# Layer 1's adaLN vectors contracted lane by lane on VectorE during the first MLP

## The chip, the cores and the metric

One NeuronCore of a Trainium2 chip runs the whole kernel. The metric is the device time of one execution in microseconds (us).

## What is computed

A two-layer diffusion block works on 512 latent tokens and 256 context tokens of 1024 features. Layer 0 mixes tokens with gated linear attention (4 heads, two directions), layer 1 with neighbourhood attention (16 heads), and each layer ends with a gated MLP (2816 hidden features, a width-3 convolution on one branch). Every sub-layer is modulated by adaLN vectors. Cut to what matters here:

```python
sc_lat, sc_ctx = silu(c), silu(c_ctx)                # two conditions of 1024 features
for i in range(2):
    mod_l = sc_lat @ ada_w[i] + ada_b[i]             # ada_w[i]: 1024 x 6144, six vectors of 1024
    mod_c = sc_ctx @ ada_w[i] + ada_b[i]
    sh1, s1, g1, sh2, s2, g2 = split(mod, 6)         # for the latents and for the context
    h = rms_norm(x) * norm1_g * (1 + s1) + sh1;  x = x + g1 * mixer(h)
    h = rms_norm(x) * norm2_g * (1 + s2) + sh2;  x = x + g2 * conv_ffn(h)
```

In layer 1 the context only feeds keys and values: of its six vectors it needs the first two. Everything is float32 in and out. Large products are made exact enough from pairs of float32r tiles (a high and a low part of each operand, three matmuls for one).

## The kernel before

The work goes through five stages on one core: the first norms and adaLN vectors (0 to about 60 us), gated linear attention with its output projection (to about 490), the MLP of layer 0 (to about 1035), neighbourhood attention (to about 1410), the MLP of layer 1. The code is a list of steps; each instruction goes to the engine that the code names, and a list scheduler orders every engine's queue by the order of the code, letting a later instruction go ahead where by its own model of the times the earlier one is not ready. Tiles come from pools with a fixed number of buffers by tag; a load is issued when a buffer of its tag comes free, all loads from SyncE's one queue (SP).

**adaLN vectors.** `ada_first` makes layer 0's first two. The other ten come from `ada_step(l, m, i)` (L152): a quarter of the contraction of vector m of layer l, which is two K-tiles of 128 input features. For each K-tile a tile `sa` of 128x1024 weights (512 KB) is loaded (L159; two buffers, shared by all of them), and four float32 matmuls (L161), each over 256 columns with the 32 columns of `cs` as weights, go to four groups of 32 columns of the array and so to four groups of 32 rows of one PSUM bank `aux`. Only two of the 32 columns of `cs` carry anything (the two conditions). The profile has each of these float32 matmuls as two records, so a K-tile is 8 records of L161. After the fourth quarter ScalarE copies 256 columns out (`rows`, L166), two transposes (L171) turn them feature major, and VectorE adds the bias (`ada_use`, L114).

**Where the steps stand.** `part_a(h)` (L603) is the first part of an attention head, called the level part here: seven levels of decay products (VectorE L491 to L498, matmuls L469), after each of the first five a group of 24 value and gate matmuls (`vr_group`), and after each level one `ada_step`. The list `blocks` (L670) has 28 of them: layer 0's vectors 2 to 5, then layer 1's vectors 0 to 2. `part_b(h)` (L618), the state part, makes the key decay (L519, L521), the key transposes (L531), the states (L542) and the outputs (L578), and between them the next head's query and key projections (`qk_group`, 24 matmuls each); at its end stands one more `ada_step` in heads 0 to 2 (L654). Head 3 has four in its level part. In the neighbourhood attention (L999 to L1065) another twelve `ada_step` calls make layer 1's vectors 3 to 5, two in each of five pairs of heads and two among the last output products.

**Weights.** `wunit` (L189) loads 128x1024 weights into `st` (L193; three buffers), ScalarE rounds them into `wh` (L200) and VectorE subtracts for `wl` (L201); five pairs of buffers.

**The MLP of layer 0** (`ffn`, L723): 22 tiles of 128 hidden features, in six groups of three and one of four. `in_tile(j)` (L763) runs the two input products over all 768 tokens (96 matmuls), and `finish` (L782) makes the convolution on VectorE (L788 to L790), the gate's SiLU on ScalarE, the gated product (L796) and the split into `uh`, `ul` (L217, L218). After a group the output products of its tiles are summed for each token tile in PSUM (`mm`, three buffers), and VectorE multiplies by the gate and adds to the residual (L293, L294). The first two tiles of the MLP are run together by `in_first` (L770).

Of the kernel before, what the change touches and what calls it, by code (L numbers as in the profile page):

```python
# [16 lines left out]
KD = 8  # L17
# [15 lines left out]
# row ranges of the packed small vectors  # L33
# [5 lines left out]
def body(ctx, tc, x, ctx_x, small, ada0, ada, w_gla, a_w1, a_w2, gn, w_go, w_fi, w_fo,  # L39
# [19 lines left out]
    # ---------------------------------------------------------------- constants  # L59
# [30 lines left out]

    sT = cst.tile([128, 384], F32, name="sT")
# [5 lines left out]
    # ---------------------------------------------------------------- adaLN vectors  # L97
# [11 lines left out]
    def ada_use(l, o, n, src):  # L109
        """Feature tiles o..o + n of layer l's adaLN vectors, from their products with the conditions."""  # L110
# [14 lines left out]
    def ada_first(q, pool):  # L125
        """256 columns (two feature tiles) of the first two adaLN vectors of layer 0; returns what is left to do."""
# [25 lines left out]
    def ada_step(l, m, i):  # L152
        """Quarter i of the contraction of adaLN vector m of layer l; returns what is left to do with it."""
# [21 lines left out]

    def gate_rows(pool, l, n, j):
# [11 lines left out]
    # ---------------------------------------------------------------- helpers  # L188
    def wunit(src, gate=None, eng=None):  # L189
        """1024 columns of weights (times a gate for each) as an exact pair of float32r tiles."""  # L190
# [29 lines left out]
    # the features that the projections read, as pairs of float32r: one place for all sub-layers  # L220
# [4 lines left out]
    def affine(i, dst, src, l, n, k, j):  # L225
        """dst = src * A + B of feature tile k, on the engine that i picks."""
# [6 lines left out]
    def normed(pool, xt, g=None, cut=(0, 512, 1024), **at):  # L233
        """xt / rms(xt) (times g), as two halves of the features."""
# [22 lines left out]
    def norm_pair(pool, l, n, t, c0, blocks=False, **at):  # L257
        """Modulated norm of token tiles t and t + 1, feature major, into columns c0.. of H; returns
        the part that TensorE begins."""
# [36 lines left out]
    # ================================================================ layer 0, GLA  # L296
# [44 lines left out]
    with tc.tile_pool(name="gla", bufs=6) as pool:  # L341
# [22 lines left out]
        # w2 as rows of (high, high, low) parts against the rows (high, low, high) of the low-rank features  # L364
# [98 lines left out]
        def blocks_of(kk, qq, w, flip):  # L463
            """Products of w keys by w queries, of the same block or (flip) of its neighbour; keys on partitions."""
# [92 lines left out]
        def silu_r(h, c):  # L557
            """norm_g * silu(r) of one chunk, with the exponential's table."""
# [44 lines left out]
        def part_a(h, extra=None):  # L603
            vr_group(h, 0)
            diag(h)
            for i in range(7):
# [8 lines left out]
                if extra and i >= 5:  # L615
                    extra(i - 5)

        def part_b(h, fill):  # L618
            """fill: up to eight callables of other work, one after each step."""
            fill = list(fill) + [None] * 8  # L620

            def other(i):
# [545 lines left out]
```

## Time and profile before

| | us |
|---|---|
| median of 3 runs | 1770.52 |
| lowest and highest run | 1769.62, 1773.61 |
| profiled execution: its span, the only time given for it | 1771.4 |
| TensorE busy | 1719.7 (97%) |
| VectorE busy | 1037.1 (59%) |
| ScalarE busy | 663.7 (37%) |
| GpSimd busy | 319.7 (18%) |

The page shows the slowest core, here the only one. PE is TensorE, PEld its weight loads, DVE VectorE, ACT ScalarE, POOL GpSimd, SP the queue of loads. Matmuls are pipelined, so the records of two neighbours overlap: what one costs is read from start to start. PEclk is the clock granted to TensorE as a share of full speed.

### The profile page before, as it was taken

What the parts mean: (1) busy time and instruction counts of PE and PEld (TensorE: products, weight loads), DVE (VectorE), ACT (ScalarE), POOL (GpSimd) and SP (SyncE); (2) the same over time, 40 slices, a digit from 0 to 9 for tenths busy, and PEclk for the clock granted to TensorE, in tenths of its full rate; (3) what the DMA queues carried; (4) which work ended last, traced back from release to release, by engine and by line L of the source; (5) the groups of instructions that cost most, each with busy time, mean ns of one, the idle gap of its engine ahead of it and who ended that gap; (6) DMA issues with size and microseconds to landing.
All of it is one profiled execution on the core that took longest, in us unless ns stands there. A gap on an engine that the chain in (4) does not pass through costs nothing.

```text
span 1771.4 us, 27345 instructions
## 1 busy us (share of the span) xinstructions
PE 1719.7 (97%) x11099; PEld 1451.4 (82%) x11099; DVE 1037.1 (59%) x1599; ACT 663.7 (37%) x1225; POOL 319.7 (18%) x474
## 2 busy tenths in 40 slices
PE   6999999999999999999999999999999999999998
PEld 4767676777798999989899978888888788888887
DVE  4697767774646455564655484445445565556555
ACT  4575646552441211212122254443434432233222
POOL 2042323221100000000000023433443202222221
PEclk9999999999999999999999999999999999999999
DMA  8553525331121211212212122133232232333331
GB/s 288 154 192 120 191 84 191 93 111 72 49 95 60 72 60 48 79 59 66 63 57 72 60 66 70 50 100 103 98 107 73 84 106 80 101 107 106 92 100 48
DMA packets 50446, 169.36 MB, mean 96 GB/s; under 512 B 6608, under 2 KB 8528, under 8 KB 50320
## 3 DMA queue, kind: packets, MB, share of 16 engines
q1 hardware_dynamic: 50320, 167.62, 29.3%
q8 instruction: 87, 1.43, 0.3%
q14 instruction: 39, 0.32, 0.1%
HBM read 163.40 MB, written 2.10 MB: 93 GB/s over the span
## 4 chain that ended last, share of the span: by engine, by line
PE 80%; DVE 9%; ACT 3%; issue 2%; DMA 2%; POOL 2%; SPq 0%; DVEq 0%; POOLq 0%; ACTq 0%
PE mm L205 18%; PE mm L206 17%; PE mm L207 17%; PE aux L205 6%; PE aux L207 6%; PE aux L206 6%; PE mm L962 2%; PE aux L945 2%; PE aux L920 2%; DVE t L498 1%; PE aux L161 1%; DVE t L497 1%; PE aux L578 1%; DVE t L492 1%; PE aux L542 1%
## 5 line engine op out<-in xcount | busy, mean ns | idle before, releaser
L205 PE MATMUL mm<-hh,wl 128*128 128x384 f32 (+3 forms) x976 | 344.0, 353 | 3.8 <-ACT hh L217 2.8
L206 PE MATMUL mm<-hl,wh 128*128 128x384 f32 (+3 forms) x976 | 340.6, 349 | 0.4 <-DVE hl L218 0.4
L207 PE MATMUL mm<-hh,wh 128*128 128x384 f32 (+3 forms) x976 | 340.6, 349 | 0.0
L200 ACT ACTIVATE wh<-st 128x1024 fp32r<-128x1024 f32 (+1 forms) x197 | 204.0, 1052 | 317.7 <-issue 179.5
L201 DVE TENSOR_TENSOR wl<-st,wh 128x1024 fp32r<-128x1024 f32 (+1 forms) x196 | 242.7, 1244 | 65.0 <-ACT wh L200 43.0
L205 PEld LDWEIGHTS mm<-hh,wl 128*128 128x128 f32 (+1 forms) x976 | 183.5, 188 | 23.6 <-ACT hh L217 3.5
L206 PEld LDWEIGHTS mm<-hl,wh 128*128 128x128 f32 (+1 forms) x976 | 183.9, 188 | 20.5 <-issue 4.2
L205 PE MATMUL aux<-hh,wl 128*128 128x384 f32 (+2 forms) x576 | 200.5, 348 | 0.0
L207 PE MATMUL aux<-hh,wh 128*128 128x384 f32 (+2 forms) x576 | 200.2, 348 | 0.0
L206 PE MATMUL aux<-hl,wh 128*128 128x384 f32 (+2 forms) x576 | 200.2, 348 | 0.0
L207 PEld LDWEIGHTS mm<-hh,wh 128*128 128x128 f32 (+1 forms) x976 | 184.0, 189 | 15.0
L205 PE MATMUL mm<-wh,ul 128*128 128x512 f32 (+1 forms) x444 | 175.1, 395 | 0.0
L206 PE MATMUL mm<-wl,uh 128*128 128x512 f32 (+1 forms) x444 | 173.7, 391 | 0.0
L207 PE MATMUL mm<-wh,uh 128*128 128x512 f32 (+1 forms) x444 | 172.8, 391 | 0.0
L197 POOL TENSOR_TENSOR st<-st,gB 128x512 f32<-128x512 f32 x60 | 92.6, 1572 | 269.2 <-DMA st<-in 177.5
L788 DVE TENSOR_SCALAR tt<-apad,sT 128x769 f32<-128x769 f32 (+1 forms) x44 | 32.3, 734 | 166.7 <-ACT apad L759 166.7
L245 POOL TENSOR_SCALAR ms<-ss 128x1 f32<-128x1 f32 x26 | 8.8, 340 | 621.0 <-ACT xn L243 620.3
L205 PE MATMUL mm<-wh,hl 128*128 128x512 f32 x288 | 117.7, 409 | 2.3 <-ACT wh L200 1.7
L206 PE MATMUL mm<-wl,hh 128*128 128x512 f32 x288 | 116.0, 403 | 0.0
L205 PEld LDWEIGHTS aux<-hh,wl 128*128 128x128 f32 x576 | 108.3, 188 | 8.9 <-issue 1.8
L207 PE MATMUL mm<-wh,hh 128*128 128x512 f32 x288 | 115.7, 402 | 0.0
L206 PEld LDWEIGHTS aux<-hl,wh 128*128 128x128 f32 x576 | 108.5, 188 | 7.5 <-issue 0.4
(200 smaller groups left out, 2779.4 us busy)
## 6 DMA issues: line engine op xcount, KB each, us to landing
st<-in SPq DMA_DIRECT2D x196, 512.0 KB, 3.6
sa<-in SPq DMA_DIRECT2D x82, 512.0 KB, 4.2
sx<-in SPq DMA_DIRECT2D x14, 512.0 KB, 5.7
xl<-in SPq DMA_DIRECT2D x8, 512.0 KB, 7.7
xc<-in SPq DMA_DIRECT2D x4, 512.0 KB, 4.7
out<-xn SPq DMA_DIRECT2D x8, 256.0 KB, 2.0
raw<-in SPq DMA_DIRECT2D x16, 96.0 KB, 2.4
t<-q SPq DMA_DIRECT2D x16, 64.0 KB, 3.6
```

The source lines that it names most:

```text
L161: mm(ps[32 * j:32 * j + 32, 0:256], cs[:, k, :], st[:, 256 * j:256 * j + 256], start=k == 0, stop=k == KD - 1, skip_group_check=True)
L197: nc.gpsimd.tensor_mul(st[:, s_], st[:, s_], gate[half])
L200: nc.scalar.activation(hi, st, AF.Copy)
L201: (eng or nc.vector).tensor_sub(lo, st, hi.bitcast(F32))
L205: mm(out, a[1], b[0], start=first, stop=False)
L206: mm(out, a[0], b[1], start=False, stop=False)
L207: mm(out, a[0], b[0], start=False, stop=last)
L492: nc.vector.tensor_sub(v(eq)[:, :, 0, :], v(bB)[:, :, 0, :], cB)
L788: nc.vector.tensor_scalar(tt, ap_[:, 1:1 + m], cw[1], cb, OP.mult, OP.add)
L920: mm(pss[hh][:, off:off + 256], qe[a_][p_, 128 * t:128 * t + 128], ke[b_][p_, ks], start=i == 0, stop=i == 2)
L945: nc.tensor.transpose(pT[:, i * 128:(i + 1) * 128], S2[:, o:o + 128], ident)
L962: mm(po[64 * hh:64 * hh + 64, 128 * t:128 * t + 128], V[:, vs[i], 64 * hh:64 * hh + 64], PTs[hh][:, i * 128:(i + 1) * 128], start=i == 0, ...
```

## The change

- Layer 1's twelve steps in the linear attention and twelve in the neighbourhood attention are removed. Layer 0's sixteen stay; a level part now has a step after its first six levels while there are any left (6, 6, 4), and the state part has none.
- New `ada_lanes(pool, l, m, c)`: eight steps, one for each K-tile. A step loads one `sa` tile and lets VectorE multiply it by the condition's value of the lane (the partition) and add it to an accumulator `acc` of 128x1024 (one buffer). The eighth step adds up the 128 lanes with one group of four float32 matmuls against `one0` (a column of ones and 31 of zeros), and goes on as `ada_step` did: copy, two transposes, bias.
- The MLP of layer 0 has a list of eight such jobs: vectors 0 and 1 for the latents and for the context, vectors 2 to 5 for the latents, 64 steps in all. Each `in_tile` runs four of them at its end, so that they fill tiles 2 to 17.
- The MLPs' pool has four instead of five buffers for tags without a number of their own.

```diff
+    one0 = cst.tile([128, 32], F32, name="one0")
+    nc.gpsimd.memset(one0, 0.0)
+    nc.gpsimd.memset(one0[:, 0:1], 1.0)
...
+    def ada_lanes(pool, l, m, c):
+        acc = [None]
+
+        def step(k):
+            if k == 0:
+                acc[0] = pool.tile([128, 1024], F32, name="acc", tag="acc", bufs=1)
+            st = ast.tile([128, 1024], F32, name="sa", tag="sa")
+            nc.sync.dma_start(st, ada[6 * l + m - 2, k])
+            if k == 0:
+                nc.vector.tensor_scalar(acc[0], st, cs[:, k, c:c + 1], None, OP.mult)
+            else:
+                nc.vector.scalar_tensor_tensor(acc[0], st, cs[:, k, c:c + 1], acc[0], OP.mult, OP.add)
+            if k < KD - 1:
+                return
+            ps = ps_aux()
+            for j in range(4):
+                mm(ps[32 * j:32 * j + 32, 0:256], one0, acc[0][:, 256 * j:256 * j + 256], start=True, stop=True,
+                   skip_group_check=True)
+            rows = sml.tile([128, 256], F32, name="rows", tag="rows", bufs=1)
+            nc.scalar.activation(rows, ps[:, 0:256], AF.Copy)
+            pm = ps_aux()
+            for f in range(2):
+                nc.tensor.transpose(pm[:, f * 128:(f + 1) * 128], rows[:, f * 128:(f + 1) * 128], ident)
...
+        return [lambda k=k: step(k) for k in range(KD)]
...
-                todo = ada_step(*blocks.pop(0)) if h < HEADS - 1 or i < 4 else None
+                todo = ada_step(*blocks.pop(0)) if blocks and i < 6 else None
...
-            if h < HEADS - 1:
-                ada_step(*blocks.pop(0))()
...
-        blocks = [(0, m, i) for m in range(2, 6) for i in range(4)] + [(1, m, i) for m in range(3) for i in range(4)]
+        blocks = [(0, m, i) for m in range(2, 6) for i in range(4)]
...
-        with tc.tile_pool(name=f"ffn{l}", bufs=5) as pool:
+        with tc.tile_pool(name=f"ffn{l}", bufs=4) as pool:
...
-                return finish(j, [in_group(j, 1, w1, rng) for rng in rngs])
+                u = finish(j, [in_group(j, 1, w1, rng) for rng in rngs])
+                for job in jobs[:4]:
+                    job()
+                del jobs[:4]
+                return u
...
+            jobs = []
+            if l == 0:
+                for m, c in ((0, 0), (0, 1), (1, 0), (1, 1), (2, 0), (3, 0), (4, 0), (5, 0)):
+                    jobs += ada_lanes(pool, 1, m, c)
...
-        later = [(1, m, i) for m in range(3, 6) for i in range(4)]
...
-            if 1 < pr < 7:
-                ada_step(*later.pop(0))()
...
-                if t in (1, 2):
-                    ada_step(*later.pop(0))()
```

## Rows read from the trace of the kernel before

**Rows 1.** The page: the span, and the busy time of each engine with its share of the span and its instructions.
```profile
span 1771.4 us, 27345 instructions
PE 1719.7 (97%) x11099; PEld 1451.4 (82%) x11099; DVE 1037.1 (59%) x1599; ACT 663.7 (37%) x1225; POOL 319.7 (18%) x474
```

**Rows 2.** Busy time by stretch: from:to and length, then busy us (instructions) of PE, PEld, DVE, ACT and POOL, the granted clock, the DMA engines' busy share and GB/s. State part of head 0, level and state part of head 1, of head 2, level part of head 3.
```profile
124.60:160.60 36.00, 35.62 (x202) 30.16 (x201) 24.77 (x35) 17.86 (x34) 9.50 (x14) 1.00 0.52 174
160.60:200.30 39.70, 37.56 (x466) 26.80 (x465) 38.95 (x64) 25.62 (x57) 12.07 (x12) 1.00 0.39 122
200.30:249.10 48.80, 45.08 (x337) 37.68 (x337) 25.81 (x38) 22.76 (x44) 10.75 (x16) 0.93 0.45 150
249.10:288.20 39.10, 37.05 (x464) 26.38 (x463) 38.33 (x63) 25.58 (x57) 13.79 (x12) 1.00 0.38 118
288.20:335.70 47.50, 44.32 (x340) 37.16 (x339) 25.96 (x39) 22.73 (x44) 10.74 (x16) 0.96 0.47 159
335.70:375.10 39.40, 37.57 (x455) 27.22 (x454) 38.72 (x64) 25.60 (x57) 12.04 (x12) 1.00 0.34 108
```

**Rows 3.** The chain that ended last, in order of time (start, us, what): where head 1's state part and head 2's level part begin.
```profile
200.26 0.87 DVE t L519
...
249.12 1.73 DVE b L415 x2
```

**Rows 4.** TensorE's instructions in order of time around the start of head 1's state part: start, us, engine, line, operation, out<-in, shape, count, and in brackets the idle time before it and what ended it.
```profile
205.03 0.44 PE L205 MATMUL mm<-hh,wl 128*128 128x384 f32 x1
...
207.73 0.34 PE L205 MATMUL mm<-hh,wl 128*128 128x384 f32 x1
211.79 1.08 PE L161 MATMUL aux<-sa,cs 128*32 128x256 f32 x8 [3.72 <-DMA sa<-in]
...
213.29 0.52 PE L207 MATMUL mm<-hh,wh 128*128 128x384 f32 x1
213.61 0.52 PE L205 MATMUL mm<-hh,wl 128*128 128x384 f32 x1
...
216.84 0.42 PE L531 MATMUL aux<-ident,t 128*128 128x128 f32 x1
```

**Rows 5.** The same for head 2, from the fifth step of its level part to its key transposes.
```profile
284.88 1.07 PE L161 MATMUL aux<-sa,cs 128*32 128x256 f32 x16
285.89 0.50 PE L205 MATMUL mm<-wh,hl 128*128 128x512 f32 x1
...
291.99 0.39 PE L161 MATMUL aux<-sa,cs 128*32 128x256 f32 x1
...
292.86 0.64 PE L469 MATMUL aux<-t,t 128*32 128x32 f32 x48
293.43 0.44 PE L205 MATMUL mm<-hh,wl 128*128 128x384 f32 x1
...
299.61 0.77 PE L161 MATMUL aux<-sa,cs 128*32 128x256 f32 x8 [3.13 <-DMA sa<-in]
...
303.96 0.71 PE L531 MATMUL aux<-ident,t 128*128 128x128 f32 x5
```

**Rows 6.** The queue of loads (SP) at the same place of head 1: start, us from the first issue to the end of the last, line, what is loaded, count.
```profile
204.26 2.33 SPq L193 DMA_DIRECT2D st<-in  x2
206.69 1.31 SPq L159 DMA_DIRECT2D sa<-in  x2
```

**Rows 7.** Busy time by stretch, columns as in rows 2: the 7 us after the wait, and the 30 after them.
```profile
211.80:218.80 7.00, 7.00 (x37) 4.85 (x38) 0.00 (x0) 1.36 (x4) 1.65 (x3) 0.55 0.74 248
218.80:248.80 30.00, 30.00 (x161) 26.13 (x160) 14.40 (x25) 12.36 (x27) 3.54 (x8) 1.00 0.33 109
```

**Rows 8.** TensorE's instructions in order of time, columns as in rows 4: a K-tile between projection matmuls, and a pair of adaLN transposes.
```profile
352.27 0.40 PE L207 MATMUL mm<-wh,hh 128*128 128x512 f32 x1
352.50 0.40 PE L205 MATMUL mm<-wh,hl 128*128 128x512 f32 x1
352.83 0.64 PE L161 MATMUL aux<-sa,cs 128*32 128x256 f32 x8
353.40 0.50 PE L206 MATMUL mm<-wl,hh 128*128 128x512 f32 x1
353.74 0.40 PE L207 MATMUL mm<-wh,hh 128*128 128x512 f32 x1
...
1392.53 0.38 PE L171 MATMUL aux<-ident,rows 128*128 128x128 f32 x2
...
1392.98 0.40 PE L207 MATMUL mm<-wh,oh 128*128 128x512 f32 x1
```

**Rows 9.** Busy time by stretch, columns as in rows 2: one pair of heads of the neighbourhood attention, and its end with the last norms.
```profile
1260.00:1304.00 44.00, 44.00 (x333) 35.32 (x335) 19.42 (x44) 15.01 (x33) 16.59 (x28) 1.00 0.27 88
...
1380.00:1410.00 30.00, 27.15 (x175) 21.24 (x174) 19.60 (x35) 14.45 (x32) 5.31 (x12) 1.00 0.33 106
```

**Rows 10.** The same for a group of three tiles of the first MLP: its input products, and its output products.
```profile
563.00:616.00 53.00, 53.00 (x303) 52.43 (x302) 24.97 (x33) 16.58 (x24) 0.00 (x0) 1.00 0.25 80
616.00:638.00 22.00, 22.00 (x96) 17.75 (x95) 15.68 (x23) 0.30 (x1) 0.00 (x0) 1.00 0.07 24
```

**Rows 11.** The instructions of L789 and of L788: engine, operation, out<-in, count, ns least/median/most, first and last start, shapes. The shorter durations belong to the 512 columns of the second MLP, the medians to 769.
```profile
L789 DVE SCALAR_TENSOR_TENSOR tt<-apad,sT,tt x44: 740/1021/1804, 515.2 to 1738.5; 128x769 f32<-128x769 f32 x22, 128x512 f32<-128x512 f32 x22
...
L788 DVE TENSOR_SCALAR tt<-apad,sT x44: 540/682/1537, 514.5 to 1737.9; 128x769 f32<-128x769 f32 x22, 128x512 f32<-128x512 f32 x22
```

**Rows 12.** VectorE's instructions in order of time at the end of the first group's input products, columns as in rows 4.
```profile
541.63 0.95 DVE L218 TENSOR_TENSOR ul<-u,uh 128x768 fp32r<-128x768 f32 x1
543.63 1.39 DVE L293 TENSOR_TENSOR tmp<-mm,gB 128x512 f32<-128x512 f32 x2 [1.06 <-PE mm L207]
```

**Rows 13.** The transfers of tile `sa`, all 82, from issue to landing.
```profile
DMA to landing us min/median/max: 3.3/4.2/6.3
```

More of the change, by code (lines that the diff above doesn't have):

```diff
@@ L174, in ada_step @@
         return turn
+    ada_jobs = []
+    def ada_lanes(pool, l, m, c):
[20 more added lines that the diff above has]
+                nc.tensor.transpose(pm[:, f * 128:(f + 1) * 128], rows[:, f * 128:(f + 1) * 128], ident)
+            o = 8 * m
+            mod = modT[l][:, o:o + 8, c]
+            bias = sT[:, R_AB + 48 * l + o:R_AB + 48 * l + o + 8]
+            nc.vector.tensor_add(mod.rearrange("p (j i) -> p j i", i=2),
+                                 pm[:, 0:256].rearrange("p (i j s) -> p j i s", i=2, j=4)[:, :, :, 0],
+                                 bias.rearrange("p (j i) -> p j i", i=2))
+            if m in (1, 4):
+                i = 0 if m == 1 else 1
+                r = (R_N1, R_N2)[i] + 8 * l
+                nc.vector.scalar_tensor_tensor(modA[l][:, 8 * i:8 * i + 8, c], mod, 1.0, sT[:, r:r + 8], OP.add,
+                                               OP.mult)
+        return [lambda k=k: step(k) for k in range(KD)]
     def gate_rows(pool, l, n, j):
@@ L1046, in body @@
             values(pr, 2)
-            if 1 < pr < 7:
-                ada_step(*later.pop(0))()
             turn(pr, 3)
@@ L1063, in body @@
                     rest()
-                if t in (1, 2):
-                    ada_step(*later.pop(0))()
     fgB = []
```

## The prediction

> **What bounds the kernel now.** I read the page's busy line first: TensorE is busy for 97% of the span, VectorE for 59% [rows 1]. So a matmul that goes away should be worth its own time, unless the stage it leaves is one of the few that another engine paces. The next view, the busy time stretch by stretch, finds that exception. Each linear-attention head has two parts. In its level part (heads 1 to 3: 39.7, 39.1 and 39.4 us) VectorE is busy for 38.95, 38.33 and 38.72 us, and the length is the same whether seven contraction steps run in it (heads 1 and 2) or four (head 3): VectorE paces it. In the state part TensorE paces, and the lengths differ: 36.0 us in head 0, 48.8 in head 1, 47.5 in head 2 [rows 2]. The boundaries are the start of the gate scan (L415) and of the key decay (L519) [rows 3].
>
> The instructions of TensorE in order of time say why heads 1 and 2 are longer. At 205.03 head 1 begins the first 24 projection matmuls of the next head; the seventh contraction step of part_a stands in the middle of them, its weights are not there, and TensorE waits 3.72 us. Then matmuls start 0.32 us apart (213.29 to 213.61) until, at 216.84, the first key transpose can go [rows 4]. The same happens in head 2: 3.13 us, and the transposes begin at 303.96 [rows 5]. The DMA queue shows the cause: the two transfers of that step were issued at 206.69, behind two weight loads (`st`) of which the second was held [rows 6]. And the granted clock was 0.55 in the 7 us after the wait, 1.00 afterwards [rows 7]: 1.2 instead of 2.4 GHz for most of them. In the neighbourhood attention and in the MLP TensorE is busy without a gap at a clock of 1.00 [rows 9, 10].
>
> **The change, part by part.** Time is counted against the profiled span, 1771.4 us; the page gives no other time of that execution, and the median of the runs, 1770.52, lies 0.9 lower.
>
> *What a contraction step costs on TensorE.* A K-tile of a step is 8 records of L161. Alone between projection matmuls it stretches two starts from 352.50 to 353.74, 1.24 us, where two pitches of 0.23 would be 0.46: 0.78 us. Without the changeovers it is 0.57 us (352.83 to 353.40) [rows 8]; two in a row take 1.01 us (284.88 to 285.89) [rows 5]. A step is two K-tiles: 1.0 to 1.6 us, and I take 1.2.
>
> *Linear attention.* Twelve of 28 steps go (layer 1's first three vectors), and the 16 left run in the first six levels of heads 0 to 2: 6, 6 and 4 instead of 8, 8, 8 and 4.
> - Head 0 loses its seventh step and the one at the end of the state part, both where TensorE paces: 2 x 1.2 = 2.4 us.
> - Head 1 loses the same two. Without the first the 24 matmuls (the first 16 go out from 205.03 to 207.73, 0.18 apart) end at 205.03 + 24 x 0.18 = 209.3, so the transposes start 7.5 us earlier than 216.84: 3.7 us of wait, the rest contraction and slow clock. With the last step, 1.2: 8.7 us.
> - Head 2 keeps four. Two of the three removed from its level part lie ahead of the transposes' matmuls (those from 284.88 and 291.99); without them the seventh level's products, now at 292.86, are over at 291.4 instead of 293.43, and 24 matmuls end at 295.7: 8.3 us before 303.96. With the last step: 9.5 us.
> - Head 3 loses four steps in a part that VectorE paces: 0.
>
> Sum 20.6 us. The bounds: 8 us if a wait like the two comes back elsewhere, 22 if head 3 gives a little. VectorE also loses three bias additions there, too short to count.
>
> What the slow clock does is in the term as rows show it. The Trainium skill, "TensorE: Matmul & The Clock Gate", section "HAM oscillation — how this bites in real kernels", tells the same story of a wait for a transfer that drops the clock, and its rule would also turn against the change: contraction work that filled gaps in the level parts is gone. By the rows those gaps do not matter: with 2.1 of 39.1 us idle in head 2 and 1.8 of 39.4 in head 3 the clock stayed at 1.00 [rows 2]. By the rule it could fall in head 3, which would idle 1.8 + 4 x 1.2 = 6.6 us; the sum of 20.6 would then shrink by what the rival of the clock, below, is priced at.
>
> *Neighbourhood attention.* Twelve steps go where TensorE is busy 44.00 of 44.00 us [rows 9]. Eleven x 1.2 = 13.2; the twelfth stands among the last norms, where TensorE has 2.85 us idle of 30 [rows 9], and counts 0. Six transposes: a pair takes 1392.98 - 1392.53 - 0.23 = 0.22 us [rows 8], 0.7 for three vectors. Sum 13.9 us, bounds 11 and 17.
>
> *First MLP, on TensorE.* Eight jobs (six vectors for the latents, two for the context), each with one group of four matmuls of the form of a K-tile, 0.78, and two transposes, 0.22: 8 x 1.0 = 8.0 us added; nothing hides them, as TensorE has no gap there [rows 10].
>
> *First MLP, on VectorE.* 64 steps over 128x1024 values. L789 is the same operation: 1.02 us for 769 columns and 0.74 for 512, so 1.09 ns a column, and 1024 take 1.30 us; the first of each job, by L788 (0.68 and 0.54), 0.82 [rows 11]. A group of three tiles lasts 75 us and has VectorE busy 40.7 [rows 10]; twelve steps add 15 us: 56 of 75. On the average it fits. GpSimd is idle there [rows 10], so nothing of its work is in the way.
>
> *The transfers.* 64 loads of 512 KB replace 48, through the same two buffers and the same queue, where a transfer takes 4.2 us (3.3 to 6.3) from issue to landing [rows 13]. Two at a time give a step every 2.7 us or so; eight need about 25 us, and a job has two tiles, 33 us, without the output products. What stands behind a waiting step on VectorE are the gated products and splits of the tile (L796, L218), the weight splits (L201) and the additions to the residual (L293, L294); behind a waiting load on the queue, the next `st`. The weights are converted well ahead of use, and the additions have three PSUM buffers, so the tender place is the end of a group: the last split ends at 541.63 + 0.95 = 542.6, and the first output sum is done at 543.6 [rows 12], a margin of 1 us. A step of 1.3 us that has just started there costs up to 0.3 us, with a wait for its transfer 2 to 3. Seven such places, and the two norms beside them: bounds 0 and 15 us, none below, since nothing in that stage is removed. I take 3, as VectorE is free a good third of the time and most steps will be over by then.
>
> *The pool of the MLP, four buffers instead of five,* and the new tiles: nothing, covered by the same gaps; if that cover failed, it would show as waits of the norms, within the bounds just given.
>
> The sum: 20.6 + 13.9 - 8.0 - 3 = 23.5 us. 1771.4 - 23.5 = 1747.9, and 0.9 less for the median: 1747 us, 1.3% faster.
>
> **The rivals.**
> - *The wait comes back.* Layer 0's remaining steps still queue their transfers behind `st` loads, and the sixth step of head 1 or one of head 2 could be the late one; or the weights of the next head become late once the transposes come earlier. For it: the cause sits in the queue, and the queue stays. Against it: the sixth step of head 2, at 291.99, had its data in time [rows 5]. The linear attention then gives 8 us or so, the rest as above: 1760.
> - *The clock falls in the level parts.* Less filler in heads 2 and 3, TensorE idles, and 144 value and gate matmuls of a head at 0.23 become 0.46 for part of the time. If a quarter of them in each of two heads runs at half speed, 2 x 36 x 0.23 = 17 us come back: 1764. Against it: the 1.00 of those parts now.
> - *VectorE becomes the bound of the MLP: slower.* A VectorE that waits inside its queue for a transfer is lost to the tile. With y us for a step and its wait, a group needs 40.7 + 12 y. Beyond y = 2.9 that exceeds 75 us, and the groups are paced by it; the time is longer than before once each of 5.3 groups loses over 5 us, from y = 3.3 on. With 1.3 of work and 2.1 of wait (half of a transfer's 4.2, as two run at a time) y is 3.4, a group loses 6.5 and all 35; the gain of 34.5 less 8.0 is 26.5. That gives 1771.4 + 35 - 26.5 - 0.9 = 1779. For it: the steps are issued just behind one another in every tile, and only two buffers feed them. Against it: it needs every step to wait in full, though the loads depend on nothing but a free buffer and can run ahead of the tile.
>
> **How the numbers follow.** The forecast has 0.62, the returning wait 0.16, the clock 0.09, VectorE as the bound 0.13. Likeliest 1747. The forecast alone ranges from 1738 (no stall, upper bounds of both attention terms) to 1755 (stalls of 10). To leave out only the slower case and some of the clock's, the range is 1738 to 1764. A measurement of this kernel can tell 0.2%, 3.5 us, from no change. Faster by more than that: the first three cases, nearly whole, 0.86; slower: 0.11; within: 0.03.
>
> **What would show it.** Right: no wait of TensorE for `sa` at the start of the state parts of heads 1 and 2, a clock of 1.00 there, state parts of some 38 to 40 us; level parts still 39 us; neighbourhood attention shorter by 14 us; no L161 after head 2; the MLP longer by 8 to 12 us with VectorE busy some 56 of 75. Wrong: waits of TensorE on L218, L796 or L293 at every group's end, idle time of VectorE ahead of the lane steps that `sa` ended, level parts at a lower clock, or a wait for `sa` or `st` as long as the two removed.

## The result and the profile after

The changed kernel takes 1756.19 us (median of 4 runs, 1750.43 to 1757.60) against 1770.07 beside it: a ratio of 0.9909, with a 95% interval of 0.9893 to 0.9925. The ratio stands for 16 us less, 0.9%, where 1747 and 1.3% were forecast; the two medians lie 13.9 us apart, and the same kernel measured once more (the last experiment) has 0.9902, 17 us. The profiled execution took 1755.54 us. Its span stands against [rows 1] as follows: TensorE lost 316 matmul records, VectorE gained 67 instructions.

```profile
span 1753.8 us, 26851 instructions
PE 1695.0 (97%) x10783; PEld 1442.9 (82%) x10783; DVE 1107.6 (63%) x1666; ACT 663.1 (38%) x1227; POOL 331.8 (19%) x476
```

**Where the time went, stage by stage.** I measured each stage from one fixed instruction to another, in both traces: the first gate scan of a head, the first key transpose, the first matmul of the gate rows behind head 3 (L182, now L227), and the first convolution step (L788, now L835) of the first and the last MLP tile.

| stretch | before, us | after, us | change | forecast |
|---|---|---|---|---|
| head 0's scan to gate rows (linear attention) | 339.4 | 322.1 | -17.3 | -20.6 |
| of it, head 0's scan to its key transposes | 48.8 | 48.8 | 0.0 | -1.2 |
| key transposes of head 0 to head 1 | 87.5 | 81.9 | -5.6 | -8.7 |
| head 1 to head 2 | 87.1 | 77.4 | -9.7 | -9.5 |
| head 2 to head 3 | 90.7 | 88.8 | -1.9 | -1.2 |
| first MLP, first to last tile | 484.4 | 500.6 | +16.2 | +11.0 |
| from there to the same place of the second MLP's start | 419.1 | 405.7 | -13.4 | -13.9 |

The forecast column of the second to fifth lines divides the terms by the instant at which each removed step stood: the last step of a head's state part stands behind its own key transposes. The first line and the last two sum to -14.5; the rest of the 17.6 us between the spans is 1.7 us ahead of the first scan and 1.4 us between gate rows and MLP. Those are differences between executions: kernels below that leave these parts as they were (e1, e2) have the second as well, and over all runs the first scan starts anywhere from 78.4 to 82.6 us.

**The linear attention.** Busy time by stretch (columns as in rows 2), to be laid beside [rows 2]; the boundaries are again scans and key decays, but the list scheduler orders them a little differently, so lengths can't be compared to the microsecond.

```profile
160.70:197.00 36.30, 34.19 (x440) 25.34 (x439) 35.45 (x58) 24.43 (x52) 16.19 (x12) 1.00 0.35 113
197.00:243.90 46.90, 43.80 (x362) 37.81 (x362) 29.20 (x44) 23.94 (x50) 13.09 (x20) 0.96 0.33 105
243.90:279.70 35.80, 34.21 (x394) 24.59 (x393) 35.51 (x58) 24.05 (x51) 12.99 (x9) 1.00 0.36 119
279.70:325.90 46.20, 42.33 (x344) 37.42 (x343) 28.64 (x42) 23.56 (x49) 13.86 (x20) 0.96 0.26 81
```

The level parts of heads 1 and 2 keep VectorE busy throughout (35.45 of 36.30, 35.51 of 35.80), and their clock is 1.00 with six and four contraction steps in them. The state parts have not become 38 to 40 us, and their clock is 0.96. TensorE's instructions at the place of [rows 4] show why:

```profile
201.43 0.34 PE L251 MATMUL mm<-hl,wh 128*128 128x384 f32 x1
203.93 0.69 PE L175 MATMUL aux<-ident,rows 128*128 128x128 f32 x2 [2.15 <-ACT rows L170]
...
205.35 0.69 PE L252 MATMUL mm<-hh,wh 128*128 128x384 f32 x1
205.83 0.52 PE L250 MATMUL mm<-hh,wl 128*128 128x384 f32 x1
...
209.53 1.47 PE L576 MATMUL aux<-ident,t 128*128 128x128 f32 x12
```

The wait of 3.72 us for `sa` is gone; the key transposes start at 209.53 instead of 216.84. But another wait stands a few microseconds earlier: 2.15 us for `rows`, which ScalarE copies out of PSUM (L170) before the adaLN transposes. Two projection matmuls behind it start 0.48 us apart (205.35 to 205.83), where 0.17 is usual here. The copy itself starts at 203.51; ScalarE has no wait of its own in the 6 us ahead of it, only other work, weight copies (L245) among it. At the place of [rows 5], head 2:

```profile
286.93 1.47 PE L576 MATMUL aux<-ident,t 128*128 128x128 f32 x12
...
288.59 0.34 PE L252 MATMUL mm<-hh,wh 128*128 128x384 f32 x1
291.92 1.63 PE L587 MATMUL aux<-V,t 128*128 128x256 f32 x4 [2.99 <-ACT t L577]
```

Here the transposes start 17 us earlier than at 303.96, and the next thing is late: the state matmuls (L587) wait 2.99 us for the copies of the transposed keys (L577), again on ScalarE. Its own instructions there:

```profile
288.25 0.40 ACT L608 ACTIVATE er<-er 128x256 f32<-128x256 f32 x1
289.82 0.42 ACT L610 ACTIVATE er<-er 128x256 f32<-128x256 f32 x1 [1.17 <-DVE er L609]
290.15 0.47 ACT L479 ACTIVATE q<-mm 128x384 f32<-128x384 f32 x1
290.52 1.62 ACT L577 ACTIVATE t<-aux 128x512 f32<-128x512 f32 x4
```

The copies start at 290.52, 3.6 us after the transposes began. Ahead of them in ScalarE's queue stood a gate operation (L610) that itself waited 1.17 us for VectorE (L609).

**The first MLP.** At the end of a group of tiles, VectorE's instructions in order of time, the place that [rows 12] showed:

```profile
671.44 1.28 DVE L195 SCALAR_TENSOR_TENSOR acc<-sa,cs,acc 128x1024 f32<-128x1024 f32 x1
672.63 1.08 DVE L843 TENSOR_TENSOR u<-tt,aux 128x256 f32<-128x256 f32 x3
675.01 1.28 DVE L195 SCALAR_TENSOR_TENSOR acc<-sa,cs,acc 128x1024 f32<-128x1024 f32 x1 [1.29 <-DMA sa<-in]
676.21 0.95 DVE L263 TENSOR_TENSOR ul<-u,uh 128x768 fp32r<-128x768 f32 x1
```

and TensorE's at the same time:

```profile
674.71 0.40 PE L250 MATMUL mm<-wh,ul 128*128 128x512 f32 x1
677.21 0.50 PE L250 MATMUL mm<-wh,ul 128*128 128x512 f32 x1 [2.10 <-DVE ul L263]
...
679.19 0.63 PE L251 MATMUL mm<-wl,uh 128*128 128x512 f32 x1
679.62 0.63 PE L252 MATMUL mm<-wh,uh 128*128 128x512 f32 x1
```

The second lane step (L195) stands ahead of the last split of the group (L263, before: L218). It waits 1.29 us for its transfer and works 1.28, and TensorE waits 2.10 us for the split. Then its matmuls start 0.43 us apart instead of 0.23. The same happens once more six tiles later (2.6 us); the other group ends have no wait. The step that waits is the eighth and last of a job, handed out at the end of one tile and run in the next. The queue of loads (columns as in rows 6) shows its transfer among three whose issuing took 6.03 us, for there are only two buffers:

```profile
670.62 6.03 SPq L191 DMA_DIRECT2D sa<-in  x3
```

On the average VectorE has room: of a group, with its input and its output products as in [rows 10],

```profile
545.00:599.00 54.00, 54.00 (x317) 52.01 (x316) 34.83 (x44) 15.10 (x24) 0.00 (x0) 1.00 0.53 164
599.00:621.00 22.00, 22.00 (x97) 17.82 (x96) 21.02 (x29) 1.25 (x2) 0.00 (x0) 1.00 0.58 174
```

it is busy 55.9 us of 76. The instructions of the two lane lines (columns as in rows 11), and the neighbourhood attention, which is as full as in [rows 9]:

```profile
L195 DVE SCALAR_TENSOR_TENSOR acc<-sa,cs,acc x56: 1274/1282/1287, 401.8 to 896.1; 128x1024 f32<-128x1024 f32 x56
...
L193 DVE TENSOR_SCALAR acc<-sa,cs x8: 752/754/755, 397.8 to 876.0; 128x1024 f32<-128x1024 f32 x8
```

```profile
1244.00:1288.00 44.00, 44.00 (x329) 36.62 (x328) 21.68 (x51) 16.30 (x35) 17.85 (x31) 1.00 0.16 50
```

### The profile page after: what moved, and what is told of

It is laid out like the page before. It is cut to its first block, busy times and chain, and to the rows that moved or that the text cites. A ratio compares the mean times of both kernels' runs of the same rounds, so it can differ in the third digit from the quotient of the medians.

```text
span 1753.8 us, 26851 instructions
## 1 busy us (share of the span) xinstructions
PE 1695.0 (97%) x10783; PEld 1442.9 (82%) x10783; DVE 1107.6 (63%) x1666; ACT 663.1 (38%) x1227; POOL 331.8 (19%) x476
## 4 chain that ended last, share of the span: by engine, by line
PE 79%; DVE 9%; ACT 4%; issue 3%; DMA 2%; POOL 2%; SPq 0%; DVEq 0%; POOLq 0%; ACTq 0%
PE mm L250 18%; PE mm L252 17%; PE mm L251 17%; PE aux L250 6%; PE aux L251 6%; PE aux L252 6%; PE mm L1013 2%; DMA sa<-in 2%; PE aux L996 2%; PE aux L971 2%; DVE t L543 1%; PE aux L623 1%; DVE t L537 1%; PE aux L316 1%; PE aux L587 1%
## 5 line engine op out<-in xcount | busy, mean ns | idle before, releaser
L245 ACT ACTIVATE wh<-st 128x1024 fp32r<-128x1024 f32 (+1 forms) x197 | 204.2, 1052 | 311.4 <-PE mm L252 171.2
L802 ACT ACTIVATE apad<-mm 128x256 f32<-128x256 f32 (+3 forms) x90 | 36.5, 433 | 208.9 <-PE mm L252 208.9
```

What stands on the lines that cost most here:

```text
L245: nc.scalar.activation(hi, st, AF.Copy)
L802: nc.scalar.activation(apad[j % 2][:, pad_of(p0):pad_of(p1 - 1) + 1], ps[:, p0 - a:p1 - a], AF.Copy)
```

## Experiments

Ratios are to the kernel before, run on the same chip; "us less" is worked out from the ratio. The labels e1 to e12 are those that the expectations use.

**The two halves, alone (e1, e2).** Where vectors are not computed, memory holds 0.5 in their place.

```diff
 before, layer 1's vectors 0 to 2 left out
...
-                todo = ada_step(*blocks.pop(0)) if h < HEADS - 1 or i < 4 else None
+                todo = ada_step(*blocks.pop(0)) if blocks and i < 6 else None
...
-            if h < HEADS - 1:
-                ada_step(*blocks.pop(0))()
...
-        blocks = [(0, m, i) for m in range(2, 6) for i in range(4)] + [(1, m, i) for m in range(3) for i in range(4)]
+        blocks = [(0, m, i) for m in range(2, 6) for i in range(4)]
```

> The kernel before with the linear attention's part of the change alone: layer 1's vectors 0 to 2 are not computed (their adaLN tiles hold a constant 0.5), everything else of layer 1 stays on TensorE as before. Theory (each stage pays its own price, the prices add up): the first MLP begins about 19 us earlier than before, as in the changed kernel, and all of it stays: about 1751. Rival (the stage's gain is partly a matter of where the profiled executions began, or is given back in the MLP): 1757 or more.

Measured: 1754.33 us, 0.9894 [0.9866, 0.9922], which is 18.8 us less. The stages agree: 320.9 us from head 0's scan to the gate rows, 18.5 less than before, and an MLP of 484.4.

```diff
 before, layer 1's vectors 3 to 5 left out
...
-            if 1 < pr < 7:
-                ada_step(*later.pop(0))()
...
-                if t in (1, 2):
-                    ada_step(*later.pop(0))()
```

> The kernel before with the neighbourhood attention's part alone: layer 1's vectors 3 to 5 are not computed (constant 0.5), the rest as before. Theory: TensorE paces the stage, so it loses 13 to 14 us and nothing else moves: about 1756.5. Rival (VectorE or ScalarE paces part of the stage, and the fill was free): 1762 or more.

Measured: 1760.37, 0.992 [0.9889, 0.9951], 14 us less. From the MLP's last tile to the second MLP it takes 405.8 us instead of 419.1, as the changed kernel does. The other stages are as long as before (339.1 us from head 0's scan to the gate rows, 484.4 for the MLP). So the term is the time in which TensorE no longer does this work, 13.3 us for twelve steps and their transposes, and the rival, that part of it was free, falls.

**The change without its price (e3), and with TensorE's part of it alone (e4).**

```diff
 after
-                for m, c in ((0, 0), (0, 1), (1, 0), (1, 1), (2, 0), (3, 0), (4, 0), (5, 0)):
-                    jobs += ada_lanes(pool, 1, m, c)
+                pass
```

> The changed kernel without the eight lane jobs: layer 1's six vectors are not computed (constant 0.5). Theory: the first MLP lasts as long as before, so the changed kernel's 16 us there are all the jobs' price: about 1740, 0.991 of the changed kernel. Rival (part of those 16 us comes from the four instead of five buffers of the MLP's pool, which stay): 1745 or more.

Measured: 1740.13, 0.9812 [0.9787, 0.9838], 33 us less; the sum of the two halves is 32.8. Its MLP takes 484.4 us, as before. So the pool of four buffers costs nothing, and all 16 us that the changed kernel's MLP is longer belong to the lane jobs.

```diff
 after: the lane jobs without loads and VectorE steps
             if k == 0:
                 acc[0] = pool.tile([128, 1024], F32, name="acc", tag="acc", bufs=1)
-            st = ast.tile([128, 1024], F32, name="sa", tag="sa")
-            nc.sync.dma_start(st, ada[6 * l + m - 2, k])
-            if k == 0:
-                nc.vector.tensor_scalar(acc[0], st, cs[:, k, c:c + 1], None, OP.mult)
-            else:
-                nc.vector.scalar_tensor_tensor(acc[0], st, cs[:, k, c:c + 1], acc[0], OP.mult, OP.add)
+                nc.gpsimd.memset(acc[0], 0.01)
```

> The changed kernel with lane jobs that load nothing and add nothing up on VectorE (the accumulator is set to 0.01); their matmuls against the ones, copies, transposes and bias additions stay. Theory: TensorE's own work is about 8 of the 16 us, and the rest is waits for VectorE at the end of two groups: about 1748, and no wait of TensorE for the split L263 there. Rival (TensorE's work is dearer than 1 us a job and the waits are a small part): 1753 or more.

Measured: 1749.24, 0.9867 [0.9837, 0.9896]. The MLP takes 492.4 us: the jobs' TensorE part costs 7.9 us, 0.99 a job. The other 8.2 us of the changed kernel are loads and VectorE steps. One window over the whole MLP (columns as in rows 2) shows both; the changed kernel:

```profile
494.00:994.70 500.70, 496.00 (x2674) 460.08 (x2673) 326.42 (x419) 117.98 (x174) 0.00 (x0) 0.99 0.39 120
```

and without loads and VectorE steps:

```profile
497.50:989.80 492.30, 492.30 (x2673) 457.79 (x2673) 266.50 (x362) 117.80 (x173) 6.69 (x7) 1.00 0.21 65
```

TensorE is idle 4.7 us of 500.7 in the first, and the clock is 0.99; in the second nothing is idle. So a little more than half of the 8.2 us is waiting, and the rest is the slow clock behind it.

That 8.2 is the number of one execution. The changed kernel measured again (e11) and two kernels with the same MLP (e7, e8) have an MLP of 498.0, 498.6 and 496.2 us, so that loads and VectorE steps cost 5.6, 6.2 and 3.8 us there. TensorE waits at the same two places in all four, 4.7, 3.7, 4.3 and 3.4 us in total, and the rest is again the clock: it fell behind both waits in the first execution, behind the first one in e11 and e7, and behind none in e8. The four waits with a slow clock behind them lasted 2.10 to 2.67 us, the other four 1.60 to 1.76. Around the two places, in e11 and in e8:

```profile
676.40:684.40 8.00, 5.86 (x19) 4.37 (x18) 5.80 (x7) 0.42 (x1) 0.00 (x0) 0.79 0.61 201
832.40:840.40 8.00, 6.40 (x29) 4.86 (x27) 6.99 (x11) 1.07 (x2) 0.00 (x0) 1.00 0.72 221
```

```profile
674.90:682.90 8.00, 6.24 (x27) 4.78 (x26) 7.15 (x9) 0.54 (x1) 0.00 (x0) 1.00 0.60 196
830.90:838.90 8.00, 6.32 (x27) 5.00 (x27) 7.29 (x10) 0.00 (x0) 0.00 (x0) 1.00 0.51 165
```

**Where the lane steps stand (e6).** The same work, dealt out otherwise: tiles 2, 3, 6, 9 and 12 hand out all eight steps of a job and the tiles between them four, so that a job's last step, which runs about one tile late, does not fall to the last tile of a group.

```diff
 after
-                for job in jobs[:4]:
+                n_jobs = 8 if j == 2 or j % 3 == 0 else 4
+                for job in jobs[:n_jobs]:
                     job()
-                del jobs[:4]
+                del jobs[:n_jobs]
```

> The changed kernel with the lane jobs at other tiles: eight steps at tile 2 and at the first tile of each group, four at the others, so that no job's first step comes free just ahead of a group's last tile. The work is the same. Theory (the two waits of 2.1 and 2.6 us for the split at the ends of the third and fifth group, with the slow clock behind them, are the 8 us between e4 and the changed kernel): no such wait, 1748. Rival (other group ends take the wait over, or it is VectorE's load and not the meeting of a step with a group's end): 1753 or more.

Measured: 1748.46, 0.9866 [0.9838, 0.9894]: the best kernel of this study that computes everything, faster than the one before and the changed one (1746.12 to 1751.70, where e11 has 1753.92 to 1760.21). Its MLP:

```profile
494.90:987.20 492.30, 492.30 (x2674) 457.83 (x2673) 323.49 (x419) 118.06 (x173) 0.00 (x0) 1.00 0.40 122
```

It is as long as without loads and VectorE steps at all. Lane steps still wait for transfers (18.0 us in 16 waits, 26.4 in 22 in the changed kernel), but TensorE has no wait in the MLP. So the 8.2 us are not the price of VectorE's work, nor of the transfers; they are two waits at two places and what the clock adds to them. The expectation has the step wrong: in the changed kernel it was the last step of a job, not the first, that stood ahead of a group's last split. First steps still stand there in this kernel (597.44, then the split at 599.25) and cost nothing.

**What the wait for `sa` was worth (e5).** The kernel before, but the seventh step of each level part reads the tile that was loaded last instead of its own weights; all contraction work stays.

```diff
 before
-            st = ast.tile([128, 1024], F32, name="sa", tag="sa")
-            nc.sync.dma_start(st, ada[6 * l + m - 2, k])
+            if load:
+                last[0] = ast.tile([128, 1024], F32, name="sa", tag="sa")
+                nc.sync.dma_start(last[0], ada[6 * l + m - 2, k])
+            st = last[0]
...
-                todo = ada_step(*blocks.pop(0)) if h < HEADS - 1 or i < 4 else None
+                todo = ada_step(*blocks.pop(0), load=i < 6) if h < HEADS - 1 or i < 4 else None
```

> The kernel before, with one thing gone: the seventh contraction step of each level part (heads 0 to 2) loads no weights and multiplies the tile loaded last again, so three quarters of vectors hold wrong sums. All matmuls stay. Theory (heads 1 and 2 lose 3.7 and 3.1 us waiting for that step's transfer, and about as much again to the clock that falls behind each wait): no wait of TensorE for sa at the start of the two state parts, clock of 1.00 there, about 11 us less, 0.994 of before. Rival (ScalarE's queue, which shows waits of 2.2 and 3.0 us at this place in the changed kernel, takes the wait over): 4 us less or fewer.

Measured: 1757.91, 0.9917 [0.9895, 0.9939], 14.7 us less. Both waits are gone; key transposes of head 0 to head 1 take 80.9 us (6.6 less) and head 1 to head 2 81.5 (5.6 less). Where the wait had dropped the clock, the trace now has

```profile
199.50:212.00 12.50, 12.50 (x184) 10.72 (x183) 12.20 (x15) 10.01 (x19) 5.21 (x6) 1.00 0.66 199
```

12.50 of 12.50 us busy at full clock. Two late transfers therefore cost 12.2 us, of which 6.85 us are the waits themselves. Removing the transfers alone gives most of what the linear attention gained by removing twelve steps (326.0 us from head 0's scan to the gate rows, 13.4 less than before, against 18.5 less in e1): what hurt was the place of the step in two queues more than its work.

**Head 3 (e7).** Do four steps there cost nothing, as I had it? All 16 steps of layer 0 run in the first four levels of heads 0 to 3.

```diff
 after
-                todo = ada_step(*blocks.pop(0)) if blocks and i < 6 else None
+                todo = ada_step(*blocks.pop(0)) if i < 4 else None
```

> The changed kernel with layer 0's sixteen steps as four in each of the four level parts instead of 6, 6 and 4. Theory (in head 1 the copy of a finished vector stands in ScalarE's queue behind weight copies and makes TensorE wait 2.2 us, with slow clock behind it; and head 3's level part, paced by VectorE, takes four steps for nothing): about 5 us less than the changed kernel, 1751. Rival (the state parts are paced by ScalarE and VectorE there, wherever the steps stand): 1755 or more.

Measured: 1757.77, 0.9917 [0.9894, 0.994]; the 1751 did not come. Heads 0 to 2 are faster together: head 3's scan comes at 320.1 us instead of 324.1. Head 3 gives it back. From its first scan to the gate rows, in the kernel before, the changed one and this one:

```profile
335.60:419.90 84.30, 76.53 (x726) 57.80 (x725) 63.29 (x105) 46.12 (x107) 24.49 (x38) 0.96 0.27 84
```

```profile
324.10:400.80 76.70, 68.08 (x651) 54.09 (x650) 62.71 (x101) 45.27 (x103) 26.68 (x37) 0.98 0.11 37
```

```profile
320.10:401.70 81.60, 74.00 (x716) 55.78 (x716) 62.63 (x104) 45.56 (x105) 27.59 (x37) 0.97 0.29 89
```

VectorE's busy time is nearly the same in all three, TensorE's is not, and the length follows TensorE: 4.9 us for four steps, 1.2 each. VectorE paces the level part, but what TensorE leaves undone in its gaps is done behind it, so that over the whole head a matmul is not free. (The clock over the head differs little: 0.96 before, 0.98 in the changed kernel, 0.97 here.)

**The new wait in heads 1 and 2 (e8, e9, e10, e12).** Four attempts to remove it. The first adds to the last kernel that the gate of the last chunk of tokens (`silu_r`) moves from the end of the level part to behind the first states:

```diff
-                if i > 0:
+                if 0 < i < 6:
                     silu_r(h, i - 1)
...
+            silu_r(h, 5)
             state(h, 1, 1)
```

> As e7, and the gate of the last chunk (five ScalarE and one VectorE instruction of silu_r) moved from the end of the level part to behind the first states. Theory (in head 2 the copies of the transposed keys, L577, come 3.0 us late because ScalarE's queue is held by that gate's instructions and a weight copy): about 4 us less than e7, 1747. Rival (the weight copies hold the queue and the gate does not matter): as e7.

Measured: 1754.46, 0.99 [0.9874, 0.9927]; 1747 was expected. Against e7 as it was measured that is 3.3 us less, but the intervals overlap, and of the 3.9 us between the two profiled executions 2.4 lie in the MLP, which the edit does not touch. The waits for the transposed keys (L577) are still there, 2.1 and 3.1 us, so the theory's reason does not show. The other three start from the best kernel; the first of them copies `rows` on VectorE instead of ScalarE, the second the transposed keys as well:

```diff
-        nc.scalar.activation(rows, ps[:, 0:256], AF.Copy)
+        nc.vector.tensor_copy(rows, ps[:, 0:256])
...
-                nc.scalar.activation(kt[:, c0 * CH:c1 * CH], ps[:, 0:(c1 - c0) * CH], AF.Copy)
+                nc.vector.tensor_copy(kt[:, c0 * CH:c1 * CH], ps[:, 0:(c1 - c0) * CH])
```

> As e6, with the copy of a finished layer 0 vector (rows, four of them) moved from ScalarE to VectorE. Theory (in head 1 that copy stood in ScalarE's queue and cost TensorE 2.2 us and as much again in slow clock): no wait of TensorE for rows in head 1, 3 to 4 us less than e6, 1744. Rival (e7, where this wait was gone, gained nothing: the transposes of head 1 are held by something else a moment later, or head 3 gives it back): as e6, 1748.

> As e9, with the copies of the transposed keys (16 of them over four heads) moved from ScalarE to VectorE too. Theory (in head 2 TensorE waits 2.3 to 3.0 us for them because ScalarE's queue stands behind a gate that waits for VectorE): that wait goes, 3 to 5 us less than e9, 1740. Rival (VectorE, itself full at this place, holds the copies as long): as e9 or slower.

Measured: 1750.55, 0.9865 [0.9849, 0.9882], and 1751.35, 0.9874 [0.9859, 0.9888], both like the best kernel; neither 1744 nor 1740 came. TensorE's waits at the two places (us in total, times, longest) in the second of them:

```profile
PE aux L175 <- DVE rows L170: 3.5, 1, 3.5
...
PE aux L587 <- DVE t L577: 4.2, 1, 4.2
```

The wait goes where the copy goes, and grows. In both kernels the copy for `rows` is late by 3.5 us on VectorE, by 2.15 on ScalarE. The last attempt takes weight splits off VectorE:

```diff
-            st[h]["w", i] = wunit(w_gla[h, i])
+            st[h]["w", i] = wunit(w_gla[h, i], eng=nc.gpsimd)
```

> As e6 (copies back on ScalarE), with the low parts of the query and key weights of heads 1 to 3 (two subtractions of 128x1024 a head) made by GpSimd instead of VectorE. Theory (after e9 and e10: it is VectorE itself, full of weight splits at the border between level and state part, that holds the gate, ScalarE's queue behind it and so TensorE): the waits of 2.2 and 2.3 us in heads 1 and 2 shrink to 1 us or less, with the slow clock behind them, 3 to 7 us less than e6, 0.984 of before. Rival (GpSimd takes longer for a subtraction and the first projections of the next head wait for their weights instead): as e6, 0.987, or slower.

Measured: 1755.37, 0.9913 [0.9897, 0.9929]; the expectation fell. The two places have waits of 2.1 and 4.2 us, where the best kernel has 2.2 and 2.3. The rival's reason does not show either: TensorE has next to no wait for the moved splits. They are slow on GpSimd, 2660 ns each on average, where VectorE takes about half (1.22 us for the one at 677.08, in the changed kernel). Six of the seven in this row are the moved ones, one stood there already (columns: busy us, mean ns | idle before, releasers):

```profile
L246 POOL TENSOR_TENSOR wl<-st,wh 128x1024 fp32r<-128x1024 f32 x7 | 18.6, 2660 | 36.4 <-ACT wh L245 19.4 <-DMA t<-k 17.0
```

**The changed kernel once more (e11)**, as the measure for those beside it:

> The changed kernel as it is, beside e9 and e10 on the same chip. Both theories: 0.991 of the kernel before, and so 8 us or more above e9.

Measured: 1755.81, 0.9902 [0.9885, 0.9919].

## Why the prediction was right, and which terms were off

- **The sign and the stages.** Each stage moved the way the sum said and, head 3 apart, for the reason that it gave. The measured gain, 16 us, is smaller than 23 by 7. Over the stages of the two profiled executions the shortfall is 5.2 us in the MLP, 3.3 in the linear attention and 0.5 in the neighbourhood attention. The time lies in the range on record, but 1 us above the 1755 at which the forecast taken alone ended: what the rivals added to the range holds it.
- **The linear attention's 17.3 for 20.6 is in part luck.** Behind head 2's key transposes 4.5 us were lost (to the gate matmuls, L399, now L444: 303.96 to 323.08 before, 286.93 to 310.60 after), which the sum did not have, and head 3 gave more than that, which it had at 0.
- **Neighbourhood attention, -13.9: measured -13.4**, and -14 alone. TensorE busy 44.00 of 44.00 [rows 9] was reason enough to price a step at its matmuls.
- **The MLP on TensorE, +8.0: measured +7.9.** The four matmuls and two transposes cost what a K-tile and a transpose pair cost in [rows 8].
- **VectorE's steps: 1.30 and 0.82 us estimated from [rows 11], measured 1.282 and 0.754**; 56 of 75 us busy, measured 55.9 of 76. The rival in which VectorE becomes the bound needed a wait at every step; 22 of the 64 waited, 1.2 us on average.
- **MLP stalls, +3: measured +8.2 in the profiled execution, 3.8 to 6.2 in three others. Mis-sized.** The place was the one I named, the last split of a group, and the wait was the 2 to 3 us that I gave it (1.6 to 2.7 over the four executions); it occurred twice in seven places. What the sum lacked is the second occurrence, and what I had read in [rows 7] and used for the linear attention only: a wait of TensorE can bring a slow clock behind it. In the 8 us around the first of the two the granted clock was

```profile
676.00:684.00 8.00, 6.79 (x23) 5.40 (x24) 6.18 (x9) 0.00 (x0) 0.00 (x0) 0.79 0.46 147
```

So 0.79 around 2.10 us of wait. The Trainium skill, "TensorE: Matmul & The Clock Gate", section "HAM oscillation — how this bites in real kernels", describes a wait for a transfer that leaves the matmuls behind it at the lower clock. The trace agrees, with 0.79 here and 0.55 in [rows 7], and here for a shorter wait than those of the page's example; in e8 the clock stayed at 1.00 behind waits of 1.76 and 1.68 us at the same places.
- **Head 0's seventh step, 1.2: wrong, it gave 0.0.** The sum has it where TensorE paces. It stood ahead of the key transposes, and these wait for VectorE's key decay (L521, now L566) in both traces, 0.38 us before and 0.94 without the step:

```profile
129.30 0.85 PE L531 MATMUL aux<-ident,t 128*128 128x128 f32 x6 [0.38 <-DVE t L521]
```

```profile
127.59 0.85 PE L576 MATMUL aux<-ident,t 128*128 128x128 f32 x6 [0.94 <-DVE t L566]
```

- **Head 0's last step and head 1's seventh, 1.2 and 7.5: 5.6 where 8.7 were expected. Mis-sized.** The rival of the returning wait came true in part. Its cause was not the one it named: the DMA queue was in time, and ScalarE's copy of `rows` was late. TensorE waited 2.15 us, and the clock was 0.85 for some microseconds behind it:

```profile
205.00:212.00 7.00, 6.95 (x68) 6.51 (x59) 3.99 (x7) 3.44 (x7) 4.46 (x6) 0.85 0.95 356
```

Head 2 met its number up to the key transposes (9.7 for 9.5) and lost 4.5 us behind them, by the wait of 2.99 us and a clock of 0.76:

```profile
290.00:297.00 7.00, 5.08 (x19) 4.82 (x20) 1.07 (x1) 2.91 (x8) 2.69 (x3) 0.76 0.39 132
```

- **Head 3, 0: wrong.** I argued from the level part alone. From its scan to the gate rows it gave 7.6 us, and four steps put back take 4.9 of them. Part of the other 2.7 is only where the scan stands: counted from the gate matmuls (323.08 and 310.60) to the gate rows it is 6.5 us, of which the sum has 1.2 for the step at the end of head 2. No run isolates the rest.
- **The clock in the level parts** stayed at 1.00 in heads 1 and 2. In head 3, with no steps left, TensorE waits 3.11 us for VectorE at 364.09, and the clock is 0.84 in the last 10.5 us of the level part (1.00 in [rows 2]):

```profile
325.90:361.50 35.60, 32.79 (x389) 25.56 (x387) 35.55 (x56) 26.53 (x53) 15.07 (x11) 1.00 0.01 1
361.50:372.00 10.50, 7.91 (x77) 6.80 (x78) 10.50 (x15) 7.78 (x16) 4.79 (x6) 0.84 0.46 151
372.00:400.80 28.80, 25.58 (x134) 20.46 (x133) 14.87 (x30) 9.99 (x31) 5.18 (x18) 1.00 0.12 42
```

So that rival did appear at one place, but VectorE is busy for 10.50 of those 10.50 us and sets their length; the head became shorter all the same.

**What stays open.** When TensorE comes earlier to the border between level part and state part, it waits 2 to 4 us there for a copy out of PSUM. Moving the copy to VectorE, moving the last gate, and taking weight splits off VectorE did not remove it. In head 2 the trace of the changed kernel shows ScalarE's queue waiting for VectorE just before, which suggests that the chain through both paces the border; in head 1 ScalarE was busy without a wait of its own. No run shows the cause of either. Further buffers for `sa`, which might have shortened the lane steps' waits, were not tried.

## What to carry to other kernels

A step that needs a transfer costs, in an engine's in-order queue, what stands behind it: place it where nothing urgent follows, and check that place at every repetition of the loop, since two of seven repetitions here cost 3.8 to 8.2 us, at worst as much as all of the added matmuls, and dealing the steps out differently gave it back. A part that another engine paces does not make added matmuls free: look at what then runs behind it. When you remove a wait, name what is late next and take only the distance to that as the gain. Price an idle TensorE with the slow clock that may follow it: here from next to nothing to some three quarters of the wait again (12.2 us for 6.85 us of waits in the linear attention, 8.2 for 4.7 in one execution of the MLP, 3.8 for 3.4 in another). One profile of a kernel shows one of these cases.

## What the runs showed of the hardware

After some short waits of TensorE its granted clock was lower, after others not. Around and behind waits of 2.10, 2.15 and 2.99 us in the changed kernel it was 0.79, 0.85 and 0.76 over 7 or 8 us, while two gaps of 1.0 to 1.1 us in head 1's level part left it at 1.00. A wait about as long as the first two need not lower it: 2.36 us in e7 (ending at 118.83) left 1.00 over the 8 us around it, and the same wait for `rows` stands beside 0.79 in the best kernel and beside 1.00 in e12:

```profile
204.14 0.44 PE L175 MATMUL aux<-ident,rows 128*128 128x128 f32 x2 [2.19 <-ACT rows L170]
202.00:210.00 8.00, 5.86 (x69) 5.65 (x70) 7.20 (x11) 4.40 (x10) 3.92 (x5) 0.79 0.89 304
```

```profile
208.14 0.44 PE L175 MATMUL aux<-ident,rows 128*128 128x128 f32 x2 [2.08 <-ACT rows L170]
206.00:214.00 8.00, 5.92 (x84) 5.62 (x84) 7.97 (x10) 5.71 (x13) 4.16 (x4) 1.00 0.70 196
```

A subtraction over 128x1024 values of 32 bits took 2.66 us on GpSimd and 1.22 on VectorE. On VectorE a multiplication by a value per lane (0.754 us for 1024 columns) was much cheaper than one with an addition of a second tile (1.282 us).
